# Weight chunks that start at eight places of a 64-byte line in turn

## The chip, the cores and the metric

The kernel runs on one core of a Trainium2 chip. The metric is the device time of one execution, in microseconds (us). The kernel before has a median of 2451.69 us (2 runs, 2451.65 to 2451.74).

## The reference

Two layers of a decoder trunk over 512 tokens of width 1024, in float32. What matters here is that nearly all of its arithmetic is a product of activations with large weight matrices, each of which is read once:

```python
for l in range(DEPTH):
    h = rms_norm(x, mix_norm_g[l])
    seg_a, seg_b, seg_c, seg_d, seg_g = split_last(h @ w_in[l], SEGMENTS)
    y_a, y_b, y_c, y_d = ...
    gates = jax.nn.sigmoid(seg_g.reshape(B, S, N_BRANCH, D))
    merged = (gates[:, :, 0] * (y_a @ p_a[l]) + gates[:, :, 1] * (y_b @ p_b[l])
              + gates[:, :, 2] * (y_c @ p_c[l]) + gates[:, :, 3] * (y_d @ p_d[l]))
    x = x + merged @ w_mix_out[l]
    ...
    x = x + o @ w_mem_o[l]
    u = rms_norm(x, ffn_norm_g[l]) @ w_ffn_in[l]
    ...
    x = x + (jax.nn.silu(gate) * val) @ w_ffn_out[l]
return rms_norm(x, final_norm_g)
```

The four mixers (two attentions, two recurrences) and the cross-attention between them are small beside these products.

## The kernel before, in words

Activations lie in SBUF with channels on the 128 partitions and 512 tokens along the row. The weights of both layers are laid out beforehand as 388 chunks of 128 x 1024 floats (`wst`, 512 KB each), in the order in which TensorE uses them.

`chunk()` (lines 473 to 485) brings one chunk in. SyncE starts its DMA into one of three `wst` buffers (line 480). ScalarE rounds it to the type float32r as `whi` (line 483), and VectorE takes the rest, `wst - whi`, as `wlo` (line 484). There are four buffers of `whi` and four of `wlo`, of 4096 bytes per partition each. The chunk numbers go round these buffers, so chunk n has the buffer n % 4. Each buffer of before begins 32 bytes after the start of a 64-byte line of SBUF, as do the buffers of the activations (the arena `ar`) and of `wst`.

Activations are split in the same way into a high and a low part, and `mm3` (lines 494 to 499) multiplies with three TensorE matmuls: high x high, low x high, high x low. Line 288 is the helper that issues each of them. There are two forms:

- `ws_run` and `ws_tile`: the weights are the stationary operand, 128 columns out of a chunk (512 bytes per partition, `sub()`), and the activations are the moving one. 8064 matmuls have a moving operand of 512 columns; 384 more (`mk`, the keys of the memory tokens) have one of 256. A chunk gives 8 such pieces, so it feeds 24 matmuls.
- `tm_tile`: the activations are stationary and 256 columns out of a chunk (1024 bytes) are the moving operand. These are 1344 matmuls: the values of the attentions and of the memory (`Cp`, `Bp`, `A`, `mv`).

So 9792 matmuls read a weight chunk. The pieces of a chunk lie 512 or 1024 bytes apart, so every piece of a chunk has the same place in a 64-byte line as the chunk itself.

The order on TensorE is set by a planner (`Weave`): dense projections in a queue, and chains of small steps (recurrences, attentions) put between them at times that it estimates. The chunks run ahead of their use, with high priority, as far as their buffers allow.

Some other tiles are used below because they are read or written at other places of a line. `ffn_fu` (128 x 514) is written from its third element on (line 1855, 8 bytes into the tile), read from there by ScalarE (line 1857), and read from its second and its first element by VectorE (lines 1859 and 1861). `cst` holds constants of several widths; its block `bones`, 128 columns, begins 8 bytes after a line's start and is the stationary operand at line 1075. `smt` holds small weights, and its block `g2`, the stationary operand at line 1078, begins 32 bytes after one.

Of the kernel before, what the change touches and what calls it, by code (L numbers as in the profile page):

```python
# [10 lines left out]
F32R = mybir.dt.float32r  # L11
# [10 lines left out]
P = 128  # L22
# [351 lines left out]
class Trunk:  # L374
# [98 lines left out]
    def chunk(self):  # L473
        nc = self.nc
        n = self.seg[0]
        assert n < self.seg[1]
        self.seg[0] += 1
        with self.tc.high_priority():
            st = self.wp.tile([P, 1024], F32, tag='wst', bufs=self.wb[0], name='wst%d' % n)
            nc.sync.dma_start(st, self.ins['wst'][n])  # L480
            hi = self.wp.tile([P, 1024], F32R, tag='whi', bufs=self.wb[1], name='whi%d' % n)
            lo = self.wp.tile([P, 1024], F32R, tag='wlo', bufs=self.wb[2], name='wlo%d' % n)
            nc.scalar.copy(hi, st)  # L483
            nc.vector.tensor_sub(lo, st, hi.bitcast(F32))  # L484
        return hi, lo
# [1518 lines left out]
```

## Time and profile before

| what | value |
|---|---|
| median of the runs | 2451.69 us |
| the profiled execution, its own time | 2449.37 us |
| span of the profiled execution | 2447.6 us |
| TensorE clock granted, mean over the span | 0.995 of full speed |

The span runs from the first to the last instruction; the 1.8 us between it and the execution's own time lie around it. PE is TensorE's matmuls, PEld its loads of the stationary operand, DVE VectorE, ACT ScalarE, POOL GpSimd and SP SyncE. A matmul's record is longer than its share of the stream, because records of matmuls that follow each other overlap; the distance from start to start is what a matmul costs.

### The profile page before, as it was taken

To read this page: it belongs to the slowest core of one execution; us is meant where nothing else is said; L and a number is where in the kernel's file an instruction comes from. 1 tells how busy PE (TensorE), PEld (TensorE's weight loads), DVE (VectorE), ACT (ScalarE), POOL (GpSimd) and SP (SyncE) were. 2 spreads that over 40 slices of the span, in tenths; PEclk is the share of its full clock that TensorE was granted. 3 is DMA by queue.
4 is the path that set the end of the run, shared out by engine and by line. 5 is a ranking of instruction groups with operands and counts; after the bars stand their busy time and mean duration, and the time that the engine had idled before them with its cause. 6 is when DMAs were issued, how large, how long until landed. Compare 5 with 4: busy or idle time off the path is not lost.

```text
span 2447.6 us, 34308 instructions
## 1 busy us (share of the span) xinstructions
PE 2396.2 (98%) x13344; PEld 1999.2 (82%) x13344; DVE 1511.7 (62%) x2730; ACT 974.1 (40%) x1728; POOL 457.2 (19%) x374
## 2 busy tenths in 40 slices
PE   8999999999999999999999999999999999999997
PEld 7878887788889888888888788877888898888886
DVE  6787357755655667367467864387566565763763
ACT  6242524444434444244352335244434354442441
POOL 0220042244010111011202200533421001110112
PEclk9999999999999999999999999999999999999998
DMA  5324334224424222322322342332243342323321
GB/s 185 102 92 150 100 111 135 67 77 148 130 99 147 69 95 95 103 95 95 130 93 80 111 145 81 125 104 82 83 152 112 101 137 69 104 86 98 102 94 61
DMA packets 89602, 259.69 MB, mean 106 GB/s; under 512 B 18144, under 2 KB 21856, under 8 KB 89440
## 3 DMA queue, kind: packets, MB, share of 16 engines
q1 hardware_dynamic: 57168, 205.81, 25.6%
q10 hardware_dynamic: 25872, 30.58, 3.8%
q0 software_dynamic: 6400, 21.11, 2.7%
q8 instruction: 105, 1.72, 0.3%
q14 instruction: 57, 0.47, 0.1%
HBM read 234.32 MB, written 23.13 MB: 105 GB/s over the span
## 4 chain that ended last, share of the span: by engine, by line
PE 92%; DVE 5%; ACT 1%; issue 1%; DMA 0%; POOL 0%; DVEq 0%; ACTq 0%; SPq 0%
PE ffn_pd L288 29%; PE A_pd L288 7%; PE Bp_pd L288 5%; PE Cp_pd L288 4%; PE gd_pd L288 4%; PE mo_pd L288 4%; PE mq_pd L288 4%; PE mix_pd L288 4%; PE ga_pd L288 4%; PE gc_pd L288 4%; PE Dp_pd L288 3%; PE Db_ps L288 3%; PE gb_pd L288 2%; PE matt_ps L288 2%; PE mv_pd L288 2%; PE mk_pd L288 2%
## 5 line engine op out<-in xcount | busy, mean ns | idle before, releaser
L483 ACT CAST whi<-wst 128x1024 fp32r<-128x1024 f32 x388 | 406.2, 1051 | 787.4 <-PE ffn_pd L288 216.2
L484 DVE TENSOR_TENSOR wlo<-wst,whi 128x1024 fp32r<-128x1024 f32 x388 | 495.1, 1279 | 214.3 <-ACT whi L483 213.1
L288 PE MATMUL ffn_pd<-xgh,whi 128*128 128x512 f32 x704 | 274.2, 390 | 0.0
L288 PE MATMUL ffn_pd<-xgh,wlo 128*128 128x512 f32 x704 | 273.9, 389 | 0.0
L288 PE MATMUL ffn_pd<-xgl,whi 128*128 128x512 f32 x704 | 273.9, 389 | 0.0
L1868 POOL TENSOR_TENSOR ffn_ft<-ffn_ft,ffn_fc 128x512 f32<-128x512 f32 x44 | 60.2, 1369 | 545.6 <-DVE ffn_fu L1854 350.3
L288 PEld LDWEIGHTS ffn_pd<-xgh,wlo 128*128 128x128 f32 x704 | 132.1, 188 | 27.5
L288 PEld LDWEIGHTS ffn_pd<-xgl,whi 128*128 128x128 f32 x704 | 132.2, 188 | 27.5
L288 PEld LDWEIGHTS ffn_pd<-xgh,whi 128*128 128x128 f32 x704 | 132.2, 188 | 27.1
L288 PE MATMUL ffn_pd<-fh,whi 128*128 128x512 f32 x352 | 136.9, 389 | 0.0
L288 PE MATMUL ffn_pd<-fl,whi 128*128 128x512 f32 x352 | 136.9, 389 | 0.0
L288 PE MATMUL ffn_pd<-fh,wlo 128*128 128x512 f32 x352 | 136.9, 389 | 0.0
L288 PE MATMUL A_pd<-xgh,whi 128*128 128x512 f32 x256 | 105.4, 412 | 0.0
L288 PE MATMUL A_pd<-xgh,wlo 128*128 128x512 f32 x256 | 100.6, 393 | 0.0
L288 PE MATMUL A_pd<-xgl,whi 128*128 128x512 f32 x256 | 100.3, 392 | 0.0
L1855 DVE TENSOR_TENSOR ffn_fu<-ffn_pd,r_rbc 128x512 f32<-128x512 f32 x88 | 60.4, 688 | 43.8 <-PE ffn_pd L288 43.7
L531 DVE TENSOR_TENSOR fl<-ffn_ft,fh 128x512 fp32r<-128x512 f32 x44 | 30.5, 693 | 90.6 <-ACT fh L530 90.6
L530 ACT CAST fh<-ffn_ft 128x512 fp32r<-128x512 f32 x44 | 27.3, 621 | 145.1 <-POOL ffn_ft L1868 145.1
L1857 ACT ACTIVATE ffn_fc<-ffn_fu,cvt 128x512 f32<-128x512 f32 x88 | 71.7, 817 | 26.5 <-DVE ffn_fu L1855 26.5
L1417 POOL TENSOR_TENSOR A_rp<-A_rp,snr 128x512 f32<-128x512 f32 x24 | 50.6, 2107 | 162.4 <-DVE A_rp L1416 160.4
L575 POOL TENSOR_TENSOR mo_sqa<-mo_sqa,mo_sqt 128x512 f32<-128x512 f32 x14 | 23.6, 1686 | 297.8 <-ACT mo_sqa L571 257.9
L288 PEld LDWEIGHTS ffn_pd<-fl,whi 128*128 128x128 f32 x352 | 66.1, 188 | 13.8
(584 smaller groups left out, 6138.7 us busy)
## 6 DMA issues: line engine op xcount, KB each, us to landing
wst<-in_wst_dram SPq DMA_DIRECT2D x388, 512.0 KB, 3.5
gb_gate<-gb_gu ACTq DMA_DIRECT2D x16, 256.0 KB, 2.1
gd_gate<-gd_gu ACTq DMA_DIRECT2D x16, 256.0 KB, 2.1
gc_gate<-gc_gu ACTq DMA_DIRECT2D x16, 256.0 KB, 2.1
pc_gu<-gc_gate POOLq DMA_DIRECT2D x16, 256.0 KB, 3.9
pd_gu<-gd_gate POOLq DMA_DIRECT2D x16, 256.0 KB, 3.0
pb_gu<-gb_gate POOLq DMA_DIRECT2D x16, 256.0 KB, 3.0
x<-in_x_dram ACTq DMA_DIRECT2D x13, 256.0 KB, 3.3
```

The costliest lines, as they stand in the source:

```text
L288: return self.te.matmul(out, lhsT, rhs, **kw)
L483: nc.scalar.copy(hi, st)
L484: nc.vector.tensor_sub(lo, st, hi.bitcast(F32))
L530: nc.scalar.copy(dst[0], src)
L531: nc.vector.tensor_sub(dst[1], src, dst[0].bitcast(F32))
L575: (eng or nc.gpsimd).tensor_add(acc[:, :n], acc[:, :n], t[:, :n])
L1417: nc.gpsimd.tensor_mul(t2, t2, self.snr)
L1855: nc.vector.tensor_mul(u[:, 2:514], ps, self.rb)
L1857: nc.scalar.activation(acc, u[:, 2:514], AF.Identity, scale=self.cv('cw2', ch), bias=self.cv('cb', ch))
L1868: nc.gpsimd.tensor_mul(th, th, cc[1])
```

## The change

Each `whi` and `wlo` buffer gets 16 floats (64 bytes) more, and chunk n begins `2 * (n % 8)` floats, that is 0, 8, ..., 56 bytes, after the start of its buffer. `whi` and `wlo` of a chunk have the same shift. All readers and writers of a chunk use the shifted view.

```diff
             st = self.wp.tile([P, 1024], F32, tag='wst', bufs=self.wb[0], name='wst%d' % n)
             nc.sync.dma_start(st, self.ins['wst'][n])
-            hi = self.wp.tile([P, 1024], F32R, tag='whi', bufs=self.wb[1], name='whi%d' % n)
-            lo = self.wp.tile([P, 1024], F32R, tag='wlo', bufs=self.wb[2], name='wlo%d' % n)
+
+            at = 2 * (n % 8)
+            hi, lo = (self.wp.tile([P, 1040], F32R, tag=x, bufs=self.wb[1 + i], name='%s%d' % (x, n))[:, at:at + 1024]
+                      for i, x in enumerate(('whi', 'wlo')))
             nc.scalar.copy(hi, st)
             nc.vector.tensor_sub(lo, st, hi.bitcast(F32))
```

The order of the instructions on each engine, their sizes and what each waits for are the same in the two programs. The eight longer buffers still begin 32 bytes into a line, so the chunks begin at 32, 40, 48, 56, 0, 8, 16 and 24 bytes into one, and one chunk in eight stands as before. Everything that was placed behind these buffers moves up by 512 bytes in all, which leaves its place in a line as it was. The longer buffers fit into SBUF with all buffer counts unchanged.

## Rows read from the trace of the kernel before

**Rows 1.** The page: busy us, share of the span, instructions.

```profile
PE 2396.2 (98%) x13344; PEld 1999.2 (82%) x13344; DVE 1511.7 (62%) x2730; ACT 974.1 (40%) x1728; POOL 457.2 (19%) x374
```

**Rows 2.** The page: the chain that ended last, by engine.

```profile
PE 92%; DVE 5%; ACT 1%; issue 1%; DMA 0%; POOL 0%; DVEq 0%; ACTq 0%; SPq 0%
```

**Rows 3.** The chain in order of time: start us, length us, piece.

```profile
742.48 23.03 PE mk_pd L288 x192
...
779.33 14.39 PE mv_pd L288 x120
...
872.21 348.20 PE ffn_pd L288 x1536
```

**Rows 4.** Waits of TensorE: us in total, times, longest us.

```profile
PE Cp_pd L288 <- ACT whi L483: 1.5, 1, 1.5
```

**Rows 5.** Waits of SyncE's DMA queue: us in total, times, longest us.

```profile
SPq L480 <- DVE wlo L484: 1892.0, 323, 33.3
```

**Rows 6.** One stretch of `ffn_pd`, 872 to 1220 us: each engine's busy us (count).

```profile
core 0: us, PE busy (x) PEld busy (x) DVE busy (x) ACT busy (x) POOL busy (x), PEclk, DMA share, GB/s
872.00:1220.00 348.00, 348.00 (x1537) 288.16 (x1537) 210.58 (x306) 133.57 (x167) 40.15 (x31) 1.00 0.31 104
```

**Rows 7.** Timeline of TensorE around 900 us: start us, length us.

```profile
899.97 0.39 PE L288 MATMUL ffn_pd<-xgh,whi 128*128 128x512 f32 x1
899.97 0.19 PEld L288 LDWEIGHTS ffn_pd<-xgl,whi 128*128 128x128 f32 x1
...
900.19 0.39 PE L288 MATMUL ffn_pd<-xgl,whi 128*128 128x512 f32 x1
900.20 0.19 PEld L288 LDWEIGHTS ffn_pd<-xgh,wlo 128*128 128x128 f32 x1
```

**Rows 8.** Timeline of the loads in `mk`: start us, length us.

```profile
743.03 0.19 PEld L288 LDWEIGHTS mk_pd<-mgl,whi 128*128 128x128 f32 x1
743.15 0.19 PEld L288 LDWEIGHTS mk_pd<-mgh,wlo 128*128 128x128 f32 x1
743.27 0.19 PEld L288 LDWEIGHTS mk_pd<-mgh,whi 128*128 128x128 f32 x1
```

**Rows 9.** Groups by form: busy us, mean ns of one | idle us before.

```profile
L288 PEld LDWEIGHTS Db_ps<-dsq,cst 128*128 128x128 f32 x8 | 1.5, 189 | 0.5 <-issue 0.2
L288 PEld LDWEIGHTS Db_ps<-dgl,smt 128*128 128x128 f32 x8 | 1.5, 189 | 1.9 <-PE gb_pd L288 1.0 <-issue 1.0
...
L288 PE MATMUL Db_ps<-dsq,cst 128*128 128x512 f32 x8 | 4.1, 592 | 0.0
L288 PE MATMUL Db_ps<-dgl,smt 128*128 128x512 f32 x8 | 4.1, 592 | 0.0
```

**Rows 10.** Groups by form, ScalarE and VectorE.

```profile
L484 DVE TENSOR_TENSOR wlo<-wst,whi 128x1024 fp32r<-128x1024 f32 x388 | 495.1, 1279 | 214.3 <-ACT whi L483 213.1
L483 ACT CAST whi<-wst 128x1024 fp32r<-128x1024 f32 x388 | 406.2, 1051 | 787.4 <-PE ffn_pd L288 216.2 <-issue 134.9 <-PE Bp_pd L288 73.5
...
L1857 ACT ACTIVATE ffn_fc<-ffn_fu,cvt 128x512 f32<-128x512 f32 x88 | 71.7, 817 | 26.5 <-DVE ffn_fu L1855 26.5
...
L1861 DVE SCALAR_TENSOR_TENSOR ffn_fc<-ffn_fu,cvt,ffn_fc 128x512 f32<-128x512 f32 x88 | 65.8, 748 | 1.2
L1859 DVE SCALAR_TENSOR_TENSOR ffn_fc<-ffn_fu,cvt,ffn_fc 128x512 f32<-128x512 f32 x88 | 65.6, 746 | 0.7 <-ACT ffn_fc L1857 0.7
L1855 DVE TENSOR_TENSOR ffn_fu<-ffn_pd,r_rbc 128x512 f32<-128x512 f32 x88 | 60.4, 688 | 43.8 <-PE ffn_pd L288 43.7
...
L533 ACT ACTIVATE xgh<-x,cvt 128x512 fp32r<-128x512 f32 x48 | 33.9, 718 | 15.3 <-DVE x L1706 8.7 <-DMA x<-in_x_dram 4.6 <-DVE x L1704 2.1
...
L531 DVE TENSOR_TENSOR fl<-ffn_ft,fh 128x512 fp32r<-128x512 f32 x44 | 30.5, 693 | 90.6 <-ACT fh L530 90.6
...
L1866 ACT ACTIVATE ffn_ft<-ffn_fc 128x512 f32<-128x512 f32 x44 | 27.2, 618 | 3.2 <-DVE ffn_fc L1861 3.2
```

## The prediction

> **What bounds the kernel now.** I read the shares of the engines first, then the chain that ended last, then that chain in order of time, then who waits for the weight chunks. TensorE is busy for 98% of the span and makes up 92% of the chain [rows 1, 2], so time is won or lost where a matmul gets shorter or longer. What one costs is read from the chain's long unbroken pieces [rows 3]. In `ffn_pd` 1536 matmuls of 512 moving columns take 348.20 us: 226.7 ns each. In `mk` 192 of 256 columns take 23.03 us: 119.9 ns each, and in `mv`, where the weights are the moving operand, 120 take 14.39 us: 119.9 ns again. The reader is to take the difference: 256 further columns cost 106.8 ns, which is 2.4 columns per ns, the upper of the clock's two levels (granted 1.00 in that stretch [rows 6]). What is left, 226.7 - 213.5 = 13.2 ns, is a fixed part of each matmul, the same for both widths. Over the 9792 matmuls that read a chunk it comes to 9792 x 13.2 = 129 us, 5.3% of the time. That is the only thing on the path that a shift of the weights could reach for the better; the columns themselves run at full clock.
>
> The making of the chunks bounds nothing. TensorE waited for a `whi` once, 1.5 us, at the start [rows 4], and the queue of the weight DMAs spent 1892.0 us waiting until `wlo` had been made from a `wst` buffer [rows 5], behind buffers that are still full: the weights stand ahead of their use.
>
> **The change part by part.** No instruction is added, removed or moved, and no wait. Only addresses differ: in 7 of 8 chunks the writes of ScalarE and VectorE, VectorE's read of `whi`, and TensorE's reads start at another place of a line than before; in the eighth they stand as they did.
>
> *ScalarE and VectorE.* Reads at other places are in the trace. VectorE reads `ffn_fu` from its second element in 746 ns and from its first in 748 ns, the same operation otherwise. ScalarE reads it 8 bytes in, in 817 ns with a scale and a bias column; a like operation with one such column takes 718 ns and with none 618 ns, so each column costs 100 ns and the shift nothing. VectorE's write 8 bytes in takes 688 ns, a write of the same size at the buffer's start 693 ns [all rows 10]. ScalarE's write at a shifted place is not shown. I bound it by the nearest rows: from 5 ns less, as VectorE's write has it, to the whole 1051 ns of the cast once more. I take zero, by VectorE's row, the nearest. Even the upper end is covered: a chunk feeds 24 x 226.7 ns = 5.4 us of matmuls, against 1.05 + 1.28 us for making it; with the cast doubled ScalarE would be busy 134 + 64 x 1.05 = 201 of the 348 us of that stretch [rows 6, 10] (1536 / 24 = 64 chunks). If that cover went, TensorE would wait for `whi`, which now happens once.
>
> *The load of shifted weights (8064 + 384 matmuls).* The nearest row is a load of the constants that begin 8 bytes into a line (`dsq,cst`) beside one of constants at 32 bytes (`dgl,smt`), equal in shape and in the matmul behind it: 189 ns and 189 ns, and the matmuls 592 and 592 ns [rows 9]. These are plain float32, not float32r. I take zero. Above, the 512-column form has room: each load starts with the matmul before it [rows 7], 227 ns ahead of its own matmul, while in `mk` the same kind of load follows every 120 ns [rows 8]. So a load could last some 107 ns longer and be hidden. In `mk` there is no such room. If a start inside a line cost a load one more fixed part there, it would be 384 x 7/8 x 13.2 = 4 us.
>
> *The moving read of shifted weights (1344 matmuls).* No row shows a float32r stream at another place. Bounds from the nearest rows: one more fixed part each, 1344 x 7/8 x 13.2 = 15.5 us, for a start that falls inside a line; or, below nothing, one place in eight that is rid of the fixed part, 9792 / 8 x 13.2 = 16 us less over all matmuls. The row of the moving stream that is nearest is `mv` at the present place, equal to `mk` where an activation streams. I take zero.
>
> The sum is nothing on 2449.37 us, the profiled execution's own time (span 2447.6 us and 1.8 us around it). The median of the runs is 2451.69 us, and I forecast that: 2452 us. With the bounds above: 2452 - 16 = 2436 and 2452 + 15.5 + 4 = 2472 us.
>
> **Rivals.**
>
> *Faster: the fixed part is a collision.* While a matmul streams, the next load reads the same partitions, and both have begun at the same place of a line in every matmul of this trace. If the 13.2 ns are what the two cost each other, and the distance between their starts decides it, 7 of 8 chunks lose it: 9792 x 7/8 x 13.2 = 113 us, 2339 us. For it speaks that the part is the same behind 512 and 256 columns, as a price per load would be, and that all matmuls of the trace share one distance, so no row refutes it. Against it: the distance does not last. The stream takes 2.4 columns per ns; the load, done within 120 ns in `mk`, takes more than 1 column per ns but has only 128 to read. By their paces, the two drift apart through every place of a line several times in one load, whatever the start. And the 348 us of `ffn_pd` hold 226.7 ns throughout while DVE, ACT, POOL and the DMAs are busy in the same memory [rows 3, 6]. A price of half the size, or at half of the places, would give 56 us, 2396 us, and still count as faster.
>
> On this the Trainium skill, "TensorE: Matmul & The Clock Gate", section "Step-by-step: what each phase is for", says that TensorE has two independent read ports into SBUF, and that loading the next weights takes no bandwidth from the running matmul. By that rule there is no collision and the time stays at 2452 us. The trace neither shows nor excludes it, since the fixed part is there whenever a load is.
>
> *Slower: the moving read falls off its pace.* In the 1344 matmuls with moving weights the stream must bring 2.4 columns per ns. If a row that starts off a boundary is fetched in twice as many accesses, each 256 columns take 106.8 ns more: at 7 of 8 places 1344 x 7/8 x 106.8 = 126 us, 2577 us; at the four odd multiples of 8 bytes alone 72 us, 2524 us. It decides from the point where 256 columns need more than their 106.8 ns, as nothing hides the stream. For it: no row has this stream at another place, and nothing has slack there. Against it: such a row is contiguous, so at most one more line is touched at its end, and the shifted reads of the two other engines cost nothing [rows 10].
>
> The skill's "SBUF — State Buffer", section "Door 1: The DMA port swizzle", gives lines of 16 bytes and asks for at least two hits in a line for full bandwidth, with a price for each crossing into a new one. By that rule an 8-byte shift leaves two floats in the first and the last line, which is just enough, and the price is at most one crossing per row. No run here shows a line's size; by the rule this rival falls away and the time is the forecast's.
>
> *Nothing reaches the read.* If TensorE fetched whole lines of 64 bytes or the shift were absorbed in some buffer, nothing would change either. This gives 2452 us like the forecast and is counted with it.
>
> **How the numbers follow.** A change under 2% can hardly be told from none here. No change, or an edge effect within the bounds 2436 to 2472 us: 0.81. The collision, whole or in part, beyond 2%: 0.11; it has a full-sized price but its mechanism fits badly. The slower stream: 0.08. The range holds the first case with some us for the spread between executions, 2430 to 2475 us; what it leaves out is the two rivals, 0.19.
>
> **What would show it.** Right: the groups of `whi` and `wlo` by form keep their means (loads 0.19 us, cast 1051 ns, subtraction 1279 ns), and the `ffn_pd` piece of 1536 matmuls stays at 348.2 us, the `mv` piece of 120 at 14.4 us. Wrong to the faster side: starts of matmuls come closer than 226.7 ns for some of the eight places, so that `ffn_pd` falls towards 1536 x 213.5 ns = 328 us. Wrong to the slower side: `mv`, `Bp` and `Cp` pieces grow while `ffn_pd` stays. If ScalarE's cast grew, TensorE's waits for `whi` would show it first.

## The result and the profile after

The changed kernel takes 2476.26 us (median of 2 runs) against 2451.69: a ratio of 1.0103, 95% interval 1.0086 to 1.012. It is slower by one per cent, 24.6 us; the interval lies clear of 1, and the time 1.3 us above the range that was given. The profiled execution has a span of 2475.1 us, 27.5 us more than before.

The page's busy line and the chain's shares, of the kernel after (answers to [rows 1, 2]):

```profile
PE 2424.9 (98%) x13344; PEld 2000.8 (81%) x13344; DVE 1512.3 (61%) x2730; ACT 973.4 (39%) x1728; POOL 456.6 (18%) x374
...
PE 92%; DVE 5%; ACT 1%; issue 1%; DMA 0%; POOL 0%; DVEq 0%; ACTq 0%; SPq 0%
```

The added time is on TensorE: PE's busy time rose by 28.7 us, and no other engine's by more than 2 us. The chain in order of time of the kernel after (start us, length us, piece; answers to [rows 3]) shows where:

```profile
751.58 22.79 PE mk_pd L288 x192
...
788.16 14.36 PE mv_pd L288 x120
...
881.79 354.35 PE ffn_pd L288 x1536
```

The 1536 matmuls of `ffn_pd` take 230.7 ns each instead of 226.7. The matmuls with 256 moving columns went the other way, a little: 118.7 ns instead of 119.9 in `mk`, 119.7 in `mv`. Adding up the times from one matmul's start to the next over the whole trace, where both read a chunk and have equal width, gives the account: 3163 matmuls of `ffn_pd` cost 12.5 us more, the 4692 other ones of 512 columns 15.8 us more, those of 256 columns 1.1 us less, and everything else 0.3 us more. The sum is 27.5 us, the whole of it.

The stretch of `ffn_pd` (busy us and count by engine, then clock and DMA; answers to [rows 6]), and the groups of the chunk's making and of one load (answers to [rows 10] and to the load in [rows 7]), after:

```profile
882.00:1236.00 354.00, 354.00 (x1537) 288.04 (x1536) 210.18 (x306) 133.29 (x167) 40.12 (x31) 1.00 0.31 102
```

```profile
L486 DVE TENSOR_TENSOR wlo<-wst,whi 128x1024 fp32r<-128x1024 f32 x388 | 495.6, 1281 | 215.3 <-ACT whi L485 213.7 <-DMA dtt<-Db_du 0.2
L485 ACT CAST whi<-wst 128x1024 fp32r<-128x1024 f32 x388 | 405.3, 1048 | 817.0 <-PE ffn_pd L288 228.7 <-issue 138.7 <-PE Bp_pd L288 75.1
...
L288 PEld LDWEIGHTS ffn_pd<-xgh,whi 128*128 128x128 f32 x704 | 132.2, 188 | 30.1
```

The reader is to see what did not change. The granted clock is 1.00 as before. The cast takes 1048 ns (1051), the subtraction 1281 (1279), the load's record 0.19 us as before. TensorE waits for a `whi` once, and the DMA queue waits as often as before, 323 times and 33.3 us at the longest; in total it is 28.6 us more than 1892.0, about as much as the kernel is longer:

```profile
PE Cp_pd L288 <- ACT whi L485: 1.4, 1, 1.4
```

```profile
SPq L480 <- DVE wlo L486: 1920.6, 323, 33.3
```

So each engine's own work is the same to some ns, and yet the same matmuls follow each other at longer intervals. What grew is the part that the prediction called fixed: 226.7 - 213.5 = 13.2 ns before, 17.2 ns on average after.

### The profile page after: what moved, and what is told of

Read it like the earlier page. It is cut to its first block, busy times and chain, and to the rows that moved or that the text cites. A ratio compares the mean times of both kernels' runs of the same rounds, so it can differ in the third digit from the quotient of the medians.

```text
span 2475.1 us, 34308 instructions
## 1 busy us (share of the span) xinstructions
PE 2424.9 (98%) x13344; PEld 2000.8 (81%) x13344; DVE 1512.3 (61%) x2730; ACT 973.4 (39%) x1728; POOL 456.6 (18%) x374
## 4 chain that ended last, share of the span: by engine, by line
PE 92%; DVE 5%; ACT 1%; issue 1%; DMA 0%; POOL 0%; DVEq 0%; ACTq 0%; SPq 0%
PE ffn_pd L288 30%; PE A_pd L288 7%; PE Bp_pd L288 5%; PE gc_pd L288 4%; PE Cp_pd L288 4%; PE gd_pd L288 4%; PE mq_pd L288 4%; PE mo_pd L288 4%; PE mix_pd L288 4%; PE ga_pd L288 4%; PE Dp_pd L288 3%; PE Db_ps L288 3%; PE gb_pd L288 2%; PE matt_ps L288 2%; PE mv_pd L288 2%; PE mk_pd L288 2%
## 5 line engine op out<-in xcount | busy, mean ns | idle before, releaser
L485 ACT CAST whi<-wst 128x1024 fp32r<-128x1024 f32 x388 | 405.3, 1048 | 817.0 <-PE ffn_pd L288 228.7
L486 DVE TENSOR_TENSOR wlo<-wst,whi 128x1024 fp32r<-128x1024 f32 x388 | 495.6, 1281 | 215.3 <-ACT whi L485 213.7
```

## Experiments

A "line" is here a block of 64 bytes of address, a way to count places; that SBUF has lines of this size, no run shows. By the chunk's place in a line, the matmuls of 512 columns in the trace after took between 227 and 233 ns in the median. Two places are at the low end, that of before (32 bytes into a line) and 24 bytes. Two things differ from place to place, though: where the weights stand in a line, and how far they stand from the activations, which all start 32 bytes into one. And the longer buffers do a third thing that the prediction passed over: they set the chunks whole lines apart, where before every weight piece and every activation row stood a multiple of 512 bytes from every other. "Distance" below is that from the start of the moving row of a matmul to the start of the row of the load that runs beside it, taken modulo 512 bytes; before, it is 0 everywhere. The traces hold the starts of the matmuls but no addresses; those follow from the order of the chunks and the places of the buffers in each program. The theories:

- A: the distance within a 64-byte line costs.
- B: the weights' own place in a line costs.
- C: the whole lines between the buffers cost.
- D, formed after the first four runs: any distance can cost, within a line or by whole lines.
- E, its rival: only a change of distance from chunk to chunk costs.

Most diffs below show the added lines alone; the lines for `hi` and `lo` that they replace are left out. A comment in a diff is not in the kernel: it says where a line stands, or what the other of two runs has in its place.

### The longer buffers alone

```diff
-            hi = self.wp.tile([P, 1024], F32R, tag='whi', bufs=self.wb[1], name='whi%d' % n)
-            lo = self.wp.tile([P, 1024], F32R, tag='wlo', bufs=self.wb[2], name='wlo%d' % n)
+            hi = self.wp.tile([P, 1040], F32R, tag='whi', bufs=self.wb[1], name='whi%d' % n)[:, 0:1024]
+            lo = self.wp.tile([P, 1040], F32R, tag='wlo', bufs=self.wb[2], name='wlo%d' % n)[:, 0:1024]
```

> The buffers of whi and wlo are 64 bytes longer, as in the changed kernel, but every chunk begins at its buffer's start: the places in a line are those of before, and only the distances by whole lines between buffers differ. Theory A (what costs is the distance, within a 64-byte line, between where the matmul's moving row starts and where the next load starts): 2452 us, ratio 1.000, and 226.7 ns from start to start in ffn_pd. Theory C (the distance by whole lines, from the longer buffers, is what costs): the whole loss of the change, 2476 us, ratio 1.010. Theory B (what costs is the weights' own place in a line): 2452 us.

Measured: 2473.0 us, ratio 1.0091 (1.0076 to 1.0106). The chain in order of time:

```profile
747.95 22.34 PE mk_pd L288 x192
...
783.94 14.12 PE mv_pd L288 x120
...
877.38 354.51 PE ffn_pd L288 x1536
```

Every chunk has its old place in a line, and `ffn_pd` has lost as much as with the whole change. Theories A and B both miss this; C alone foretold it.

### The eight places alone

```diff
+            at = 2 * (n % 8)
+            hl = self.wp.tile([P, 2176], F32R, tag='whl', bufs=4, name='whl%d' % n)
+            hi, lo = hl[:, at:at + 1024], hl[:, at + 1024:at + 2048]
```

> whi and wlo of a chunk lie in one tile of 2176 floats, so that all chunks stay a multiple of 512 bytes apart but for the shift of 0 to 56 bytes, as before the change: the eight places alone, without the 64-byte steps from buffer to buffer. Theories A and B: 2476 us, ratio 1.010, ffn_pd pieces of 1536 matmuls 354 us. Theory C: 2452 us, ratio 1.000.

The diff is against the changed kernel. Measured: 2478.78 us, ratio 1.0118 (1.0101 to 1.0135).

```profile
879.55 356.13 PE ffn_pd L288 x1536
```

C misses here: the places cost as much without the whole lines. Either part of the change does the damage alone, and the two do not add up (0.9% and 1.2%, together 1.0%).

### Weights and activations moved by 32 bytes together

```diff
         pad = self.sp.tile([P, 8], F32, name='pad')
         nc.vector.memset(pad, 0.0)
+        pad2 = self.wp.tile([P, 8], F32, name='pad2')
+        nc.vector.memset(pad2, 0.0)
```

> The chunk code of before; a tile of 32 bytes ahead of the weight buffers moves wst, whi, wlo, the small tiles and the activations all by 32 bytes: weights and activations at the start of a line, their distance 0 as before. Theory A: 2452 us, ratio 1.000. Theory B: place 0 of the changed kernel cost 6 ns per matmul of 512 columns in its trace, so 8064 x 6 = 48 us more, 2500 us, ratio 1.020.

Measured: 2451.05 us, ratio 0.9999 (0.999 to 1.0008).

```profile
744.69 23.03 PE mk_pd L288 x192
...
781.54 14.39 PE mv_pd L288 x120
...
874.39 348.21 PE ffn_pd L288 x1536
```

All three pieces are those of before to 0.01 us [rows 3]. The other place costs nothing when both operands have it; theory B falls.

### The activations moved alone

```diff
         pad = self.sp.tile([P, 8], F32, name='pad')
         nc.vector.memset(pad, 0.0)
+        pad2 = self.sp.tile([P, 8], F32, name='pad2')
+        nc.vector.memset(pad2, 0.0)
```

> The chunk code of before; a tile of 32 bytes behind the weight buffers moves the activations alone by 32 bytes: weights at their place of before, distance 32 bytes for all chunks. Theory A: the chunks at distance 32 in the changed kernel's trace took 233.0 ns per matmul of 512 columns, 6.3 more, and about 2 ns less for 256 columns: 8064 x 6.3 - 1728 x 2 = 47 us more, 2499 us, ratio 1.019. Theory B: the weights have not moved, 2452 us, ratio 1.000.

Measured: 2491.02 us, ratio 1.0164 (1.0149 to 1.0179).

```profile
752.27 22.40 PE mk_pd L288 x192
...
788.37 14.20 PE mv_pd L288 x120
...
882.19 358.40 PE ffn_pd L288 x1536
```

The same 32-byte tile, put between weights and activations instead of ahead of both, costs 1.6%, although no chunk has moved. The cause is the distance between weights and activations. As defined above it is 480 bytes here for the 512-column form: the load's row begins 32 bytes ahead of the moving row. `ffn_pd` takes 358.40 us / 1536 = 233.3 ns, 6.6 ns more than before; and the matmuls of 256 columns got shorter, 116.7 ns in `mk`. The expected 2499 us was too high: by the starts, the 4692 matmuls of 512 columns outside `ffn_pd` lost 24.1 us, 5.1 ns each instead of the 6.3 expected.

These two runs alone leave a rival: the moved rows could meet the accesses of the other engines or of the DMAs, and not TensorE's other operand. The starts in this trace speak against it, as the cost is there with and without them. In the first layer's `ffn_pd`, 266 matmuls beside which VectorE, ScalarE and GpSimd ran nothing took 233.4 ns in the mean, and 282 beside which VectorE and ScalarE ran all the time took 233.3. Over both layers, 1685 matmuls without any DMA packet under way took 233.3 ns, and 1194 with packets all the time 233.4.

### Two maps: within a line by 4 bytes, and by whole lines

```diff
+            at = n % 16          # the other run: at = 16 * (n % 8)
+            hl = self.wp.tile([P, 2176], F32R, tag='whl', bufs=4, name='whl%d' % n)
+            hi, lo = hl[:, at:at + 1024], hl[:, at + 1024:at + 2048]
```

> whi and wlo of a chunk in one tile, chunk n shifted by n % 16 floats, 4 bytes apart: sixteen distances within a line, none of whole lines. A map for one look. If the distance of the starts counts with a period that no run has left yet (theory D: any distance but a multiple of 512 bytes costs a 512-column matmul up to 6.7 ns), all fifteen shifted places lie between 226.7 and 233.3 ns from start to start and place 0 at 226.7; ratio about 1.011. If the cost comes from crossing an 8-byte boundary, the odd floats stand out above the even ones.

> The same tile, chunk n shifted by 64 bytes times n % 8: whole lines alone, whi and wlo at the same distance. Theory D: place in a line is not what counts, so seven of eight distances cost as the bytes did, 228 to 233.3 ns, ratio 1.008 to 1.012. Theory A (distance within a line): 226.7 ns throughout, 1.000.

Measured, one run each: 2480.96 us and 2469.31 us, beside 2450.36 us (median of the kernel before on the same chip). The pieces of `ffn_pd` are 356.47 and 354.39 us long. From the starts in the two traces, the mean per matmul of 512 columns in `ffn_pd`, by distance: 0 bytes 228.0 ns, 4 bytes 232.5, 8 bytes 230.5, 28 bytes 234.9, 60 bytes 230.7, the others between 230.6 and 233.8. By whole lines:

| distance, bytes | 0 | 64 | 128 | 192 | 256 | 320 | 384 | 448 |
|---|---|---|---|---|---|---|---|---|
| ns | 228.5 | 232.9 | 232.0 | 229.7 | 227.9 | 233.1 | 232.2 | 229.7 |

Distances that are 256 bytes apart agree to 0.6 ns. Odd multiples of 4 bytes do not stand out as a group. Theory A falls: whole lines are not free. Theory D's guess that place 0 would stand at 226.7 missed: there it is 228. The starts show why: after a chunk with another distance it takes some five to eight matmuls until about 227 ns are back.

The trace of the changed kernel adds that 0 and 256 bytes are not the only free distances. Its chunks at 24 bytes into a line have the distances 120 (`whi`) and 376 (`wlo`), and their matmuls in `ffn_pd` take 227.0 ns in the mean; the chunks with 32 and 288 take 232.8.

### One whole line, and four, for all chunks

```diff
+            at, to = 16, 1040    # the other run: 64, 1088
+            hl = self.wp.tile([P, 2176], F32R, tag='whl', bufs=4, name='whl%d' % n)
+            hi, lo = hl[:, at:at + 1024], hl[:, to:to + 1024]
```

> Every chunk 64 bytes behind its place of before: one whole line, the same for all chunks, so nothing changes from chunk to chunk. Theory D (the distance counts, and whole lines are not free): 512-column matmuls at the 233.3 ns of the alternating 231 and 236 seen for this distance, 8064 x 6.6 = 53 us more, less 1344 x 2 + 384 x 2 = 3.5 us for 256 columns: 2501 us, ratio 1.020. Theory E (only a change of distance from chunk to chunk costs, any constant distance by whole lines settles at 226.7 ns): 2451 us, 1.000.

> Every chunk 256 bytes behind its place of before, constant. Theory D with the distance 256 as good as 0 (227.9 ns in the mixed runs, with the settling at the chunk's start): 226.7 ns in ffn_pd, 2451 us, 1.000. If the free distances are multiples of 512 alone, up to 8064 x 6.6 = 53 us more, ratio up to 1.02.

Measured: 2485.59 us, 1.0139 (1.0125 to 1.0153), and 2447.44 us, 0.9983 (0.9974 to 0.9992). The chain of the first, then that of the second:

```profile
751.23 21.77 PE mk_pd L288 x192
...
786.64 14.14 PE mv_pd L288 x120
...
880.42 358.40 PE ffn_pd L288 x1536
```

```profile
744.38 23.03 PE mk_pd L288 x192
...
781.23 14.38 PE mv_pd L288 x120
...
874.06 348.20 PE ffn_pd L288 x1536
```

A distance of one line, the same for all, costs the very 358.40 us that 32 bytes cost; four lines cost nothing. Theory E falls, since a constant distance costs, and D stands in the form that some distances cost and some do not. As in the run with the activations moved, the matmuls of `ffn_pd` lost what was expected and the time rose by less (34 us instead of 50). The second kernel's 0.2% below before has no counterpart in these pieces. Its profiled execution was the slowest of its ten, and the span of 2448.2 us is not below that of before; I take the 0.2% as the difference that two builds with equal work can show, and read other gains of that size from the trace alone.

### Half of a load

```diff
-        mm(out, wl[0], wr[1], start=False, stop=False)
+        if wr[1].shape[-1] == 512:
+            mm(out[0:64], wl[0][:, 0:64], wr[1], start=False, stop=False)
+        else:
+            mm(out, wl[0], wr[1], start=False, stop=False)
```

> Addresses of before. The second of the three matmuls (high weights x low activations) of the 512-column form loads 64 weight columns instead of 128 and so leaves out half of the outputs' low part of that product. If the fixed 13.3 ns are lost to the load that runs beside the stream, the matmul beside the half load (the first of the three) has about half of it, 220 ns, the others 226.7. If they are a price of changing weights, whatever the load's length, all stay at 226.7 ns.

Measured, one run: 2468.82 us. The load groups by form (busy us, mean ns of one | idle us before) and the piece of `ffn_pd`:

```profile
L288 PEld LDWEIGHTS ffn_pd<-xgh,wlo 128*128 128x128 f32 x704 | 132.1, 188 | 66.6
L288 PEld LDWEIGHTS ffn_pd<-xgl,whi 128*64 128x64 f32 x704 | 94.5, 134 | 29.7
```

```profile
876.58 352.95 PE ffn_pd L288 x1536
```

Both expectations miss. The half load is shorter, 134 ns instead of 188, and still all three matmuls got slower: 228.9 ns beside the half load, 230.5 and 230.0 the two others (means of the starts in `ffn_pd`). So the 13.2 ns did not act as a price per loaded byte alone, nor as a fixed price of changing weights. The run does not tell the shorter load from the other thing that it changes, a matmul that uses 64 of the array's columns between matmuls that use 128. That the 13.2 ns depend on how the regular sequence of loads and streams falls is my reading; no run shows it.

### Two versions meant to beat both kernels

The chunks of 512-column matmuls keep distance 0, those with 256 moving columns get another one. The first version (the diff leaves out the lines that reset `self.at`):

```diff
+        self.at = 16 if name == 'mk' else 0      # in open()
...
+        self.at = 112                            # in tm_chunks()
...
+            at = self.at
+            hl = self.wp.tile([P, 2176], F32R, tag='whl', bufs=4, name='whl%d' % n)
+            hi, lo = hl[:, at:at + 1024], hl[:, at + 1024:at + 2048]
```

The second puts `whi` 48 floats and `wlo` 1136 floats into that tile for both kinds of chunk.

> Chunks of 512-column matmuls stay at distance 0 (multiples of 512 bytes). Chunks whose matmuls have 256 moving columns are shifted so that the load starts 64 bytes ahead of the moving row (448 bytes for moving weights, 64 bytes for mk). In the run with longer buffers such distances gave 114 to 115.6 ns instead of 120. Theory D with its other sign for 256 columns: 1344 x 5 + 384 x 5.8 = 9 us less, 2442 us, ratio 0.996. If the shorter times there came from the mixture of distances, not from this one: 2451 us, 1.000.

> Chunks of 512-column matmuls at distance 0. Chunks with 256 moving columns: whi at distance 320 and wlo at 64 (moving weights), whi at 192 and wlo at 448 (mk), as such pairs gave 114.7 to 115.6 and 113 to 114 ns in the run with longer buffers. 1344 x 4.9 + 384 x 6.3 = 9 us less than before, 2442 us, ratio 0.996; the version with one distance of 64 for both had 0.997, and 116.6 and 117.8 ns.

Measured: 2444.27 us, 0.9971 (0.996 to 0.9982), and 2443.27 us, 0.9965 (0.9952 to 0.9977). The chain of the first and of the second:

```profile
743.44 22.61 PE mk_pd L288 x192
...
871.51 348.21 PE ffn_pd L288 x1536
...
1985.66 13.61 PE mv_pd L288 x120
```

```profile
742.50 22.61 PE mk_pd L288 x192
...
870.59 348.20 PE ffn_pd L288 x1536
...
1981.69 13.61 PE mv_pd L288 x120
```

Both are faster than the kernel before, by 0.3%: `ffn_pd` as before, `mv` 13.6 us instead of 14.4. By the starts, the matmuls of 256 columns save 5.3 us in either version, about half of the 9 us expected; the rest of the 6 to 8 us measured is no larger than the second constant-distance kernel's unexplained 4 us. In `mk` the distance of 64 bytes gives 117.8 ns here, where it gave 113.4 ns when all chunks had it. The second version's mixed distances brought no more than the first's.

## Why the prediction was wrong, point by point

**What bounds the kernel** was right. TensorE's stream was the only thing that could move, the chunks' making is still hidden, and the whole 27.5 us lie in starts of matmuls that follow each other.

**ScalarE and VectorE at nothing** was right: 1048 and 1281 ns, at shifted places.

**The load of shifted weights at nothing** is the step that failed. It was argued from a load of float32 constants 8 bytes into a line [rows 9], and from the room of 107 ns that a longer load would have. Both are true and beside the point. The load did not get longer (188 ns), and its place alone costs nothing, as the run with everything moved by 32 bytes shows. What counts is the distance of the weights' row from the row that streams. The constants' rows did not show it; those matmuls are plain float32, a different form. The upper bound had no term for these 8064 matmuls, since I held a longer load to be the only way in which they could lose. They lost 4.0 ns each in `ffn_pd` and 3.4 ns elsewhere, 28.3 us by the starts. None of the signs of being wrong let `ffn_pd` grow, either. That the time came out only 1.3 us above the range is luck: the range was made of other terms.

**The moving read of shifted weights at nothing** was right to 1 us, with the other sign: `mv` and the like became a little faster.

**The fixed part** was not fixed. For 512 columns it is 13.2 ns at the constant distances 0 and 256 bytes and 19.8 ns at 64 and 480 bytes; for 256 columns it was between 6.6 and 13.2 ns at constant distances. The sum 9792 x 13.2 ns treated as one quantity what depends on addresses.

**The rival "collision"** had the right cause and the wrong direction. It said that the distance between the two starts decides, and that before the change all matmuls share one distance; the first is what the two 32-byte tiles show. It took this one distance for the worst, when for 512 columns it is among the best of those seen. I argued against it that the load and the stream drift apart through every place of a line anyway; the runs refute what that argument concludes. A slower case by this rival was missing: since nothing in the trace told whether distance 0 was good or bad, it belonged on both sides.

On this the Trainium skill, "TensorE: Matmul & The Clock Gate", section "Step-by-step: what each phase is for", has the load take nothing from the running matmul. Here the load's address, against that of the moving row, changes how soon matmuls follow each other, by 6.6 ns in 226.7 at a constant distance, so for float32r operands in this sequence the measurement decides against the rule as I used it. By what path the two meet, the runs do not say.

**The rival "slower"** (moving read off its pace) fell: `mv` did not grow. The Trainium skill's lines of 16 bytes ("SBUF — State Buffer", "Door 1: The DMA port swizzle") were no help either way: a distance of 64 bytes, four whole such lines, costs as much as one of 4 (232.9 and 232.5 ns).

**Overlooked**: the 64 bytes by which the buffers grew. I said that the place in a line stays and did not ask what else the spacing sets. Alone it costs 0.9%.

What stays open is the mechanism beneath the distance: why 0 and 256 bytes give 226.7 ns and 64 and 480 bytes 233.3, and why 256 columns prefer other distances. A period of 256 bytes fits the map by whole lines, but of two constant distances 256 bytes apart only 0 and 256 were run. Nor do the runs fully tell the load beside a matmul from that matmul's own weights, since all weights move together against the activations.

## What to carry to other kernels

Where a long sequence of matmuls takes its loads and its moving rows from buffers of round sizes, their distance in SBUF is a hidden parameter: padding a buffer, or a small tile allocated between weights and activations, can cost time without one instruction changing, here 0.9 to 1.6%. Before trusting that an address is neutral, move both operands together and then one alone by 32 bytes; a difference between the two shows the distance at work. A part of a matmul that is the same in every row of a trace is not thereby fixed, for all of those rows may share one condition. And the distance that suits one form of matmul need not suit another: here 64 bytes cost the 512-column form 6.6 ns and spared `mk` up to 6.5.

## What was not expected of the hardware

- Two different distances cost the same: constant 64 and 480 bytes both give 233.3 ns in the mean for 512 columns, where 0 and 256 give 226.7. The step of 6.6 ns is near the 6.7 that 16 columns take at 2.4 per ns; whether that is more than chance, no run shows. For 256 columns the means lie between 113.4 and 120.0 ns.
- The sequence seems to have a memory. In `mk` the distance of 64 bytes held 113.4 ns for 192 matmuls when the matmuls before it had that distance as well (21.77 us), and 117.8 ns when they had distance 0 (22.61 us).
- A shorter load did not help its neighbours: with 134 instead of 188 ns for one load in three, 1536 matmuls took 352.95 us instead of 348.20.
